# RWKV-7 recurrence: output products split in two places and accumulated in PSUM banks opened by products of zeros

## The chip, the cores and the metric

The kernel runs on one core of a Trainium2 chip. The metric is the device time of one execution in microseconds (us), a median over runs. TensorE (PE) does matrix products in the order of its program; VectorE (DVE), ScalarE (ACT) and GpSimd (POOL) do element-wise work; SyncE (SP) and ACT issue the DMA transfers. SBUF is the on-chip memory, PSUM the memory, in banks, into which PE writes its products.

## The reference

One hybrid decoder layer on 512 tokens of width 1024: a normalisation, one combined input projection, two mixers side by side (RWKV-7 with 16 heads of 64, and a sparse attention whose queries, keys and values come from the same projection), gates, an output projection and a gated MLP. The change is in the recurrence of the first mixer:

```python
def step(state, inp):
    r_t, w_t, k_t, v_t, a_t, b_t = inp
    sa = jnp.einsum('bhvk,bhk->bhv', state, a_t)
    state = (state * w_t[:, :, None, :] + sa[..., None] * b_t[:, :, None, :]
             + v_t[..., None] * k_t[:, :, None, :])
    return state, jnp.einsum('bhvk,bhk->bhv', state, r_t)
```

## The kernel before

All of it is one program; a scheduler decides in which order each engine's instructions stand.

**The recurrence.** It isn't stepped token by token. The 16 heads are two groups of eight (`g` = 0, 1), a group is four pairs (`GP` = 4, index `i`) of two halves (`h`), and the 512 tokens are eight chunks of 64 (`c`). For each group `recur` (L618) first finishes the inverse of each chunk's 64x64 triangular matrix from 32x32 blocks: `x` and `TT` are loaded from DRAM (L623 to L626), `mt` products (L635) are copied into `x` (ACT L639 for h = 0, DVE L641 for h = 1), and `mm` products (L649) are copied into `TT` (L654, L656). Then the chunks follow, each a chain:

- W: eight products of the state S (L687) into `xw`; DVE adds LV (L690). Chunk 0 has no state, its W is LV.
- TT: eight products of W (L701) into `xw` and `xs`; DVE (L703) and ACT (L704) copy the two halves into UV.
- BKT: eight products of UV (L710) into `xs`; DVE adds the decayed state SD (L715) and has the next state.

The outputs of a chunk are eight products of the state that it started from (L671, not for chunk 0) and eight of the chunk's own UV with GS (L674), both into `y`; each region of 128x64 is opened by its first product (`start=True`). `outputs` (L663) does them for chunk c-1, behind the W products of chunk c. Two `y` banks hold four chunks; behind every odd chunk ACT copies two half banks into YT (L678). The `y` banks take turns with `mt`'s and `mm`'s second halves in the PSUM tag `py`; `xw` and `xs` are in `px`.

**What runs beside it.** `drive` (L412) steps a list of other work (`fill`) and the spawned generators in turn. While group 1's recurrence runs, the fill is projections for the attention: `v`, then `khl` for the keys `ksp0` and `kwp0` (L823), then `qproj` q0 to q3 (L852); q4 and later follow in another list. Each is 24 products of 128x512 (L269, L270, L271: high times high, low times high, high times low) into one PSUM bank of the tag `pj`, which has two. `khl` empties its bank with two copies on ACT (L830, into `k0h` and `k1h`) and two subtractions on DVE (L831, into `k0l` and `k1l`). The weights come through three buffers each (`WB` = 3): raw, high part (ACT L109) and low part (POOL).

**Where the tiles lie.** Pool `rl` holds constants of the first mixer (`mask`, `rmask`, `sel`, `onesr`, `ltw`, `lta` and paddings). It is closed (`rtx.close()`, L813) right behind `rt1 = core(1)`, which only spawns group 1's recurrence. Pool `nk` (L814), with `k0h`, `k0l` and so on, is opened in its place. The framework orders an instruction that writes a reused place behind the last reader of the tile that lay there before.

Of the kernel before, what the change touches and what calls it, by code (L numbers as in the profile page):

```python
# [10 lines left out]
F32 = mybir.dt.float32  # L11
F32R = mybir.dt.float32r
AF = mybir.ActivationFunctionType
# [19 lines left out]
GP = 4  # L33
# [4 lines left out]
PADH, PADL, PADU, PADR = 96, 112, 80, 64  # L38
# [3 lines left out]
def hybrid_layer(ctx: ExitStack, tc: tile.TileContext, a, out, dbg=None, stop=None):  # L42
    nc = tc.nc
    te, ve, sc, po, sy = nc.tensor, nc.vector, nc.scalar, nc.gpsimd, nc.sync

    def pool(name, side="left", c=None):
        p = tc.tile_pool(name=name, bufs=1, side=side, reuse_waits="tile")
        if c is None:
            return p
        return c.enter_context(p)  # L50
# [6 lines left out]
    def pj(name):  # L57
        return ps.tile([128, 512], F32, tag="pj", name=name, bufs=2)

    def px(name):  # L60
        return ps.tile([128, 512], F32, tag="px", name=name, bufs=2)

    def py(name):
        return ps.tile([128, 512], F32, tag="py", name=name, bufs=2)
# [9 lines left out]
    def dump(name, ap):  # L74
        if dbg is not None and name in dbg:
            sy.dma_start(dbg[name], ap)

    rcx, rtx, rax, rhx, nctx, ncx = (ExitStack() for _ in range(6))
    rl = pool("rl", c=rtx)
# [218 lines left out]
    onesr = rl.tile([128, 128], F32R, name="onesr")  # L298
    ltw = rl.tile([128, S], F32R, name="ltw")
    lta = rl.tile([128, S], F32R, name="lta")  # L300
    rl.tile([128, PADR], F32, name="rpad1")
    lg1h = rc.tile([128, S], F32R, name="lg1h")
    lg1l = rc.tile([128, S], F32R, name="lg1l")
    lg2 = rc.tile([96, S], F32R, name="lg2")
# [29 lines left out]
    onesb = wp.tile([128, 128], F32, tag="raw", name="onesb", bufs=WB)  # L334
    sy.dma_start(onesb, a["onesb"])
    sc.activation(onesr, onesb, AF.Copy)
    dump("gates", gates)
    cp = pool("cp", "right", ncx)
    kcs = con.tile([128, 4, 2, 32], F32R, name="kcs")
# [278 lines left out]
    def recur(gr, g):  # L618
# [24 lines left out]
        for q in range(GP // 2):  # L643
            pm = [p_(f"mm{g}{q}{h}").rearrange(gi, i=2, j=32) for h, p_ in enumerate((px, py))]
            for i in range(2):
                for c in range(8):
                    for h in range(2):
                        lo, up = slice(64 * h, 64 * h + 32), slice(64 * h + 32, 64 * h + 64)
                        te.matmul(pm[h][lo, i, c], x1[up, 0, 2 * q + i, c], TT[up, 2 * q + i, c, 32:64], start=True,  # L649
                                  stop=True)  # L650
# [6 lines left out]
        YT = gr.YT = rh_.tile([128, 4, GP, 2, 64], F32, tag="XB", name=f"YT{g}", bufs=2)  # L657
        yield
        hs = [slice(0, 64), slice(64, 128)]
        iv = "p (i v) -> p i v"  # L660
        yps = [None]

        def outputs(c, Sc):  # L663
            if c % 4 == 0:
                yps[0] = [py(f"y{g}{c}{h}").rearrange("p (a i v) -> p a i v", i=GP, v=64) for h in range(2)]
            y = [b[:, c // 2 % 2] for b in yps[0]]
            for q in range(GP // 2):
                four = [(0, 2 * q), (1, 2 * q + 1), (0, 2 * q + 1), (1, 2 * q)]
                if c:
                    for h, i in four:  # L670
                        te.matmul(y[h][hs[(c + i) % 2], i], gr.AR[i][hs[h], 1, c * 64:(c + 1) * 64], Sc[hs[h], i],  # L671
                                  start=True, stop=False)
                for h, i in sorted(four):
                    te.matmul(y[h][hs[(c + i) % 2], i], gr.GS[:, 1 + i, c, h, :], gr.UV[:, c, i, h, :],  # L674
                              start=c == 0, stop=True)
            if c % 2:
                for h in range(2):
                    sc.activation(YT[:, c // 2, :, h], y[h], AF.Copy)  # L678

        St = None  # L680
        prev = None
        for c in range(8):
            xw, xs = px(f"xw{g}{c}"), px(f"xs{g}{c}")
            if c:
                for i in range(GP):
                    for h in range(2):
                        te.matmul(xw[hs[h], i * 64:i * 64 + 64], gr.AR[i][hs[h], 0, c * 64:(c + 1) * 64],  # L687
                                  St[hs[h], i], start=True, stop=True)
                W = rh_.tile([128, GP, 64], F32, tag="W", name=f"W{g}{c}", bufs=1)
                ve.tensor_tensor(W, xw[:, 0:64 * GP].rearrange(iv, v=64), gr.LV[:, :, c, :], op=OP.add)  # L690
                if c < 7:
                    SD = rh_.tile([128, GP, 64], F32, tag="SD", name=f"SD{g}{c}", bufs=1)
                    po.tensor_tensor(SD, St, gr.Dc[:, :, c, None].to_broadcast([128, GP, 64]), op=OP.mult)
            else:
                W = gr.LV[:, :, 0, :]
            if prev:
                outputs(*prev)
            yield
            for i in range(GP):
                for h in range(2):  # L700
                    te.matmul((xw, xs)[h][0:64, 256 + i * 64:320 + i * 64], TT[hs[h], i, c, :], W[hs[h], i], start=True,  # L701
                              stop=True)
            ve.tensor_copy(gr.UV[0:64, c, :, 0, :], xw[0:64, 256:512].rearrange(iv, v=64))  # L703
            sc.activation(gr.UV[0:64, c, :, 1, :], xs[0:64, 256:512].rearrange(iv, v=64), AF.Copy)  # L704
            yield
            prev = c, St
            if c < 7:
                for i in range(GP):
                    for h in range(2):
                        te.matmul(xs[hs[h], i * 64:i * 64 + 64], gr.BKT[i][:, c, hs[h]], gr.UV[:, c, i, h, :],  # L710
                                  start=True, stop=True)
                SN = rh_.tile([128, GP, 64], F32, tag="S", name=f"S{g}{c + 1}", bufs=2)
                xsv = xs[:, 0:64 * GP].rearrange(iv, v=64)
                if c:
                    ve.tensor_tensor(SN, xsv, SD, op=OP.add)  # L715
                else:
                    ve.tensor_copy(SN, xsv)
                St = SN
                yield
        outputs(*prev)  # L720

    def finish(gr, g):
        st = rh_.tile([128, 2, GP, 8], F32, tag="gst", name=f"gst{g}", bufs=1)
# [62 lines left out]
    def core(g):  # L786
        return spawn(invert(G[g], g), 0, 1.0), spawn(recur(G[g], g), RD, RR)
# [9 lines left out]
    for g in range(2):  # L797
        group_tiles(g)
        for i in range(GP):
            p = GP * g + i  # L800
# [276 lines left out]
    for p8 in range(8):  # L1077
        v = values(p8, os_[p8])
# [201 lines left out]
    with pool("ff") as ff:  # L1280
        ah = ff.tile([128, 22, S], F32R, name="ah")
        al = ff.tile([128, 22, S], F32R, name="al")
        for j in range(22):
            us = []
            for x in range(2):
                blk = 2 * j + x
                if blk < NU:
                    p = pu4[blk]
                    half_up(blk, 1)
                else:  # L1290
                    wh, wl = split_w(a["up"][blk], f"up{blk}")
                    p = pj(f"pu{blk}")
# [131 lines left out]
```

## Time and profile before

| | |
|---|---|
| median of three runs | 1249.28 us (1246.48 to 1250.75) |
| the profiled execution | 1244.42 us |
| its span, first to last instruction | 1242.4 us |
| mean granted TensorE clock | 0.977 of full |
| PE busy | 1191.7 us, 96% of the span |
| DVE, ACT, POOL busy | 48%, 46%, 45% |

The profile is one execution, and its times count from the start of its span. A row of the timeline gives start, length, engine, source line, operation, result <- operands, the shape, how many records, and in brackets the idle time ahead with what ended it. PE's records overlap, since products are pipelined: the distance from one start to the next is what a product costs. A float product is recorded twice, so eight products are 16 records. The granted clock is given as a share of full speed in stretches of time.

### The profile page before, as it was taken

How to read it: one execution, taken by the hardware profiler on the slowest of the kernel's cores; microseconds unless marked ns; L12 is line 12 of the kernel's file. 1: busy time of each engine (PE TensorE's matmuls, PEld its weight loads, DVE VectorE, ACT ScalarE, POOL GpSimd, SP SyncE). 2: the span in 40 equal slices, each digit the busy share in tenths (PEclk: the TensorE clock that was granted, in tenths of full speed). 3: DMA queues.
4: the chain of work that ended last, by engine and by line, in shares of the span. 5: the costliest groups of instructions: out<-in, count | busy, mean ns of one | idle time of the engine just before them, and what ended most of it. 6: DMA issues, size and time to landing. Idle time of an engine off the chain costs nothing.

```text
span 1242.4 us, 19852 instructions
## 1 busy us (share of the span) xinstructions
PE 1191.7 (96%) x7414; PEld 947.1 (76%) x7414; DVE 595.8 (48%) x1195; ACT 571.4 (46%) x1141; POOL 555.9 (45%) x519
## 2 busy tenths in 40 slices
PE   8999989999899999988999999999999999999997
PEld 6887778877677787766666766788888888888886
DVE  4225554623445393147788886745433333331103
ACT  5445553332545533246666664534444444443321
POOL 4357654433765551346323221441256565554440
PEclk8999999988989999889999999999999999999999
DMA  6522234630233347244542212761133333334421
GB/s 221 134 62 84 87 91 143 166 91 15 71 112 96 113 147 180 90 111 145 170 123 82 77 43 81 232 215 53 52 96 100 94 96 98 100 96 127 136 68 68
DMA packets 108610, 135.61 MB, mean 109 GB/s; under 512 B 46625, under 2 KB 49505, under 8 KB 108258
## 3 DMA queue, kind: packets, MB, share of 16 engines
q1 hardware_dynamic: 92306, 118.88, 32.3%
q10 hardware_dynamic: 16208, 15.47, 4.0%
q8 instruction: 58, 0.95, 0.3%
q14 instruction: 38, 0.31, 0.1%
HBM read 109.87 MB, written 21.23 MB: 106 GB/s over the span
## 4 chain that ended last, share of the span: by engine, by line
PE 53%; DVE 7%; issue 2%; POOL 2%; ACT 1%; DMA 1%; DVEq 0%; ACTq 0%; SPq 0%; POOLq 0%
PE pu L187 6%; PE pu L185 6%; PE pu L186 6%; PE dn L1156 3%; PE dn L1157 3%; PE dn L1155 3%; PE o L1021 3%; PE pt L113 3%; PE ub L1051 2%; DVE XL L608 2%; PE ub L1050 2%; PE ub L1049 2%; PE q L269 1%; PE wo L1227 1%; PE wo L1228 1%
## 5 line engine op out<-in xcount | busy, mean ns | idle before, releaser
L1297 DVE SCALAR_TENSOR_TENSOR u<-pu,cvec,u 128x511 f32<-128x511 f32 x44 | 33.0, 750 | 101.8 <-ACT u L1296 101.8
L1303 DVE TENSOR_TENSOR al<-u,ah 128x512 fp32r<-128x512 f32 x22 | 23.8, 1081 | 45.3 <-ACT ah L1302 45.3
L1301 POOL TENSOR_TENSOR u<-u,u 128x512 f32<-128x512 f32 x22 | 28.3, 1288 | 38.4 <-DVE u L1298 37.5
L1021 PE MATMUL o<-PT,vt 128*64 128x384 f32 (+3 forms) x256 | 42.8, 447 | 1.0 <-DVE PT L1009 1.0
L608 DVE TENSOR_TENSOR XL<-XL,TM 128x30 f32<-128x30 f32 (+14 forms) x60 | 42.1, 701 | 2.2
L606 DVE TENSOR_TENSOR TM<-XL 128x30 f32<-128x30 f32 (+14 forms) x60 | 23.9, 399 | 29.2 <-ACT XL L601 27.2
L1009 DVE COPY PT<-pt 128x384 f32<-128x384 f32 (+1 forms) x48 | 28.7, 598 | 15.3 <-PE pt L113 10.3
L1296 ACT ACTIVATE u<-pu,cvec 128x512 f32<-128x512 f32 x44 | 33.6, 763 | 5.2 <-PE pu L1261 5.2
L1007 ACT ACTIVATE PT<-pt 128x384 f32<-128x384 f32 (+1 forms) x48 | 25.0, 521 | 23.1 <-PE pt L113 16.1
L1298 DVE SCALAR_TENSOR_TENSOR u<-pu,cvec,u 128x510 f32<-128x510 f32 x44 | 33.0, 749 | 1.6
L567 PEld LDWEIGHTS g<-AR,KB 64*128 64x128 f32 x256 | 20.6, 187 | 14.1 <-issue 9.4
L567 PE MATMUL g<-AR,KB 64*128 64x128 f32 x256 | 23.9, 288 | 7.7 <-DVE KB L535 6.5
L1021 PEld LDWEIGHTS o<-PT,vt 128*64 128x64 f32 x256 | 15.4, 136 | 20.5 <-issue 10.4
L1203 DVE TENSOR_TENSOR p2tm<-dn,gb 128x512 f32<-128x512 f32 x4 | 2.8, 692 | 51.2 <-ACT p2jl L1201 51.2
L570 DVE TENSOR_TENSOR GS<-g,mask 128x512 f32<-128x512 f32 x32 | 20.7, 684 | 11.1 <-PE g L567 11.1
L704 ACT ACTIVATE UV<-xs 64x256 f32<-64x256 f32 x16 | 6.0, 377 | 41.3 <-PE xs L701 40.0
L294 DVE SCALAR_TENSOR_TENSOR V<-v,vec,V 128x511 f32<-128x511 f32 x8 | 6.0, 749 | 38.8 <-ACT V L293 38.8
L911 POOL TENSOR_SCALAR rh<-dist 128x512 f32<-128x512 f32 x16 | 10.1, 628 | 31.7 <-DVE stt L946 23.0
L1302 ACT ACTIVATE ah<-u 128x512 fp32r<-128x512 f32 x22 | 13.9, 633 | 21.6 <-POOL u L1301 21.6
L703 DVE COPY UV<-xw 64x256 f32<-64x256 f32 x16 | 6.6, 415 | 32.7 <-PE xw L701 18.3
L1227 PE MATMUL wo<-woh,mh 128*128 128x512 f32 x52 | 20.4, 393 | 0.0
L1228 PE MATMUL wo<-wol,mh 128*128 128x512 f32 x52 | 20.3, 390 | 0.0
(2787 smaller groups left out, 4305.4 us busy)
## 6 DMA issues: line engine op xcount, KB each, us to landing
gtd<-gt ACTq DMA_DIRECT2D x16, 256.0 KB, 2.1
qs<-qd SPq DMA_DIRECT2D x32, 128.0 KB, 3.2
g<-gtd SPq DMA_DIRECT2D x16, 256.0 KB, 3.6
xt<-in_x_dram SPq DMA_DIRECT2D x4, 512.0 KB, 5.4
bvd<-bv SPq DMA_DIRECT2D x8, 256.0 KB, 3.3
bvl<-bvd SPq DMA_DIRECT2D x8, 256.0 KB, 2.8
oad<-y SPq DMA_DIRECT2D x8, 256.0 KB, 3.4
t<-oad SPq DMA_DIRECT2D x8, 256.0 KB, 3.3
```

The costliest lines, as they stand in the source:

```text
L113: return te.transpose(o, i, ident)
L185: te.matmul(p, wh(k), mh(k), start=first and k == 0, stop=False)
L186: te.matmul(p, wh(k), ml(k), start=False, stop=False)
L187: te.matmul(p, wl(k), mh(k), start=False, stop=last and k == n - 1)
L567: te.matmul(gh[h][:, j * 128:(j + 1) * 128], KB[hs, c].rearrange("p s t -> p (s t)"), AR[hs, :, c * 64:(c + 1) * 64], start=True, stop=True)
L608: ve.tensor_tensor(XU[:, j + 1:32, 0:j], XU[:, j + 1:32, 0:j], tm, op=OP.add)
L1021: te.matmul(po8[e * 64:e * 64 + 64, j * 128:], vt[:, j, b * 256 + g * 64:b * 256 + g * 64 + 64], PT[j, e], start=False, stop=b == 1 and j ...
L1155: te.matmul(acc[half, t], sh[:, k, tsl], wh[kk], start=k == 0, stop=False)
L1156: te.matmul(acc[half, t], sh[:, k, tsl], wl[kk], start=False, stop=False)
L1157: te.matmul(acc[half, t], sl[:, k, tsl], wh[kk], start=False, stop=k == n - 1)
L1296: sc.activation(u, p, AF.Identity, scale=cvec[:, cv + 2:cv + 3], bias=cvec[:, cv + 3:cv + 4])
L1297: ve.scalar_tensor_tensor(u[:, 1:], p[:, :S - 1], cvec[:, cv + 1:cv + 2], u[:, 1:], op0=OP.mult, op1=OP.add)
```

## The change

`outputs` is replaced by two functions. `from_state(c)` does the eight state products of chunk c itself (L677), behind the W products of the same chunk (L695). `from_chunk(c)` does the eight products with GS (L683), behind the BKT products of the same chunk (L717). No region is opened by its own first product any more: `ybank` opens each of the two banks of four chunks with one product of zeros, 128x512 (L670), and all others accumulate. ACT copies whole banks (L687, 128x512) once per four chunks instead of half banks per two. The zeros are a new tile `zr` of 128x32 in pool `rl`, cut out of a padding there and filled by one ACT instruction (L338). `recur` yields once more at its end.

```diff
@@ -298,7 +298,8 @@
-    rl.tile([128, PADR], F32, name="rpad1")
+    zr = rl.tile([128, 32], F32R, name="zr")
+    rl.tile([128, PADR - 32], F32, name="rpad1")
@@ -334,6 +335,7 @@
     sc.activation(onesr, onesb, AF.Copy)
+    sc.activation(zr, onesb[:, 0:32], AF.Copy, scale=0.0)
@@ -658,27 +660,33 @@
-        yps = [None]
-
-        def outputs(c, Sc):
-            if c % 4 == 0:
-                yps[0] = [py(f"y{g}{c}{h}").rearrange("p (a i v) -> p a i v", i=GP, v=64) for h in range(2)]
-            y = [b[:, c // 2 % 2] for b in yps[0]]
-            for q in range(GP // 2):
-                four = [(0, 2 * q), (1, 2 * q + 1), (0, 2 * q + 1), (1, 2 * q)]
-                if c:
-                    for h, i in four:
-                        te.matmul(y[h][hs[(c + i) % 2], i], gr.AR[i][hs[h], 1, c * 64:(c + 1) * 64], Sc[hs[h], i],
-                                  start=True, stop=False)
-                for h, i in sorted(four):
-                    te.matmul(y[h][hs[(c + i) % 2], i], gr.GS[:, 1 + i, c, h, :], gr.UV[:, c, i, h, :],
-                              start=c == 0, stop=True)
-            if c % 2:
+        ys = {}
+
+        def ybank(c):
+            if c // 4 not in ys:
+                ys[c // 4] = []
                 for h in range(2):
-                    sc.activation(YT[:, c // 2, :, h], y[h], AF.Copy)
+                    b = py(f"y{g}{c}{h}")
+                    te.matmul(b, zr[:, 0:1].to_broadcast([128, 128]), zr[:, None, :].to_broadcast([128, 16, 32]), start=True, stop=False)
+                    ys[c // 4].append(b.rearrange("p (a i v) -> p a i v", i=GP, v=64))
+            return [b[:, c // 2 % 2] for b in ys[c // 4]]
+
+        def from_state(c, Sc):
+            y = ybank(c)
+            for h, i in [(0, 0), (1, 1), (0, 1), (1, 0), (0, 2), (1, 3), (0, 3), (1, 2)]:
+                te.matmul(y[h][hs[(c + i) % 2], i], gr.AR[i][hs[h], 1, c * 64:(c + 1) * 64], Sc[hs[h], i],
+                          start=False, stop=False)
+
+        def from_chunk(c):
+            y = ybank(c)
+            for h, i in itertools.product(range(2), range(GP)):
+                te.matmul(y[h][hs[(c + i) % 2], i], gr.GS[:, 1 + i, c, h, :], gr.UV[:, c, i, h, :],
+                          start=False, stop=c % 4 == 3 and i >= GP - 2)
+            if c % 4 == 3:
+                for h in range(2):
+                    sc.activation(YT[:, c // 4 * 2:c // 4 * 2 + 2, :, h], ys[c // 4][h], AF.Copy)
@@ -693,8 +701,8 @@
-            if prev:
-                outputs(*prev)
+            if c:
+                from_state(c, St)
@@ -703,7 +711,6 @@
-            prev = c, St
@@ -716,8 +723,8 @@
                 St = SN
-                yield
-        outputs(*prev)
+            from_chunk(c)
+            yield
```

The scheduler's order changes beyond these lines. The numbers in a name are those of the group and the chunk: `y140` is group 1, the bank opened at chunk 4, half 0; `xs14` is group 1, chunk 4.

On PE, in group 1, this stands behind the last product of `kwp0` before: q0's 24 products, of which the last three are shown, then thirteen of the 32x32 `mt` products, then q1.

```order
L269 MATMUL q0_4509<-hh_109,q0h1_4516 128x512
L270 MATMUL q0_4509<-hl_110,q0h1_4516 128x512
L271 MATMUL q0_4509<-hh_109,q0l1_4517 128x512
L635 MATMUL mt100_4589<-x11_4574 32x32 x13
L269 MATMUL q1_4555<-hh_109,q1h0_4556 128x512
L270 MATMUL q1_4555<-hl_110,q1h0_4556 128x512
L271 MATMUL q1_4555<-hh_109,q1l0_4557 128x512
```

The same place in the changed program, from the last product of `kwp0` on:

```order
L271 MATMUL kwp0_4466<-hh_109,kwp0l1_4474 128x512
L637 MATMUL mt100_4591<-x11_4576 32x32 x16
L637 MATMUL mt110_4627<-x11_4576 32x32 x16
L651 MATMUL mm100_4669<-TT1_3010,x11_4576 32x32 x16
L651 MATMUL mm110_4705<-TT1_3010,x11_4576 32x32 x16
L709 MATMUL xw10_4748<-LV1_3009,TT1_3010 64x64 x4
L637 MATMUL mt101_4592<-x11_4576 32x32 x16
L637 MATMUL mt111_4628<-x11_4576 32x32 x16
L651 MATMUL mm101_4670<-TT1_3010,x11_4576 32x32 x16
L651 MATMUL mm111_4706<-TT1_3010,x11_4576 32x32 x16
L670 MATMUL y100_4804<-zr_400 128x512
L683 MATMUL y100_4804<-UV1_3008,GS1_3003 64x64 x4
```

No product of q stands among them now, nor among those of chunks 0 to 3 that follow. The first comes in the middle of chunk 4, behind that chunk's TT products and half of its output products:

```order
L709 MATMUL xw14_5026<-W14_5036,TT1_3010 64x64
L709 MATMUL xs14_5027<-W14_5036,TT1_3010 64x64
L683 MATMUL y140_5040<-UV1_3008,GS1_3003 64x64 x4
L269 MATMUL q0_4511<-hh_109,q0h0_4512 128x512
L270 MATMUL q0_4511<-hl_110,q0h0_4512 128x512
L271 MATMUL q0_4511<-hh_109,q0l0_4513 128x512
```

All 96 products of q0 to q3 then stand in one run ahead of chunk 4's BKT products; 16 of q4 are interleaved with the rest of the recurrence (before, from chunk 4's BKT products to the end: 12 products of q).

On DVE the low parts of the keys stood ahead of the recurrence's copies (`x11<-mt101` follows two rows behind these):

```order
L831 TENSOR_TENSOR k0l_4028<-ksp0_4419,k0h_4027 64x512
L831 TENSOR_TENSOR k1l_4030<-ksp0_4419,k1h_4029 64x512
L831 TENSOR_TENSOR k0l_4028<-kwp0_4464,k0h_4027 64x512
L831 TENSOR_TENSOR k1l_4030<-kwp0_4464,k1h_4029 64x512
L841 SCALAR_TENSOR_TENSOR q0zl_4550<-q0_4509,q0zh_4549 128x512
L703 COPY UV1_3006<-xw10_4746 64x4x64
```

They now stand in chunk 4, behind its W; in brackets are the engines that a row waits for:

```order
L722 TENSOR_TENSOR S14_5014<-xs13_4975,SD13_4986 128x256 [waits PE_49,Activation_49,Pool_49]
L698 TENSOR_TENSOR W14_5036<-xw14_5026,LV1_3009 128x256 [waits DVE_49,PE_49]
L838 TENSOR_TENSOR k0l_4030<-ksp0_4421,k0h_4029 64x512 [waits PE_49,Activation_49]
L838 TENSOR_TENSOR k0l_4030<-kwp0_4466,k0h_4029 64x512 [waits Activation_49]
L711 COPY UV1_3008<-xw14_5026 64x4x64 [waits PE_49]
L838 TENSOR_TENSOR k1l_4032<-ksp0_4421,k1h_4031 64x512 [waits Activation_49]
L838 TENSOR_TENSOR k1l_4032<-kwp0_4466,k1h_4031 64x512 [waits Activation_49]
```

The first of them waits for PE besides ACT. `zr` begins 7432 bytes into pool `rl` (512 + 2048 + 8 + 256 + 512 + 2048 + 2048, the tiles ahead of it); in pool `nk` that place belongs to `k0l` (4096 to 8192), and the last reader of `zr` is the product `y141<-zr` at group 1's chunk 4. On ACT the copies into `k0h` and `k1h` (L837) stand behind the two bank copies of chunk 3 (L687), right behind `UV<-xs13`.

More of the change, by code (lines that the diff above doesn't have):

```diff
@@ L660, in recur @@
         iv = "p (i v) -> p i v"
-        yps = [None]
-        def outputs(c, Sc):
-            if c % 4 == 0:
-                yps[0] = [py(f"y{g}{c}{h}").rearrange("p (a i v) -> p a i v", i=GP, v=64) for h in range(2)]
-            y = [b[:, c // 2 % 2] for b in yps[0]]
-            for q in range(GP // 2):
-                four = [(0, 2 * q), (1, 2 * q + 1), (0, 2 * q + 1), (1, 2 * q)]
-                if c:
-                    for h, i in four:
-                        te.matmul(y[h][hs[(c + i) % 2], i], gr.AR[i][hs[h], 1, c * 64:(c + 1) * 64], Sc[hs[h], i],
-                                  start=True, stop=False)
-                for h, i in sorted(four):
-                    te.matmul(y[h][hs[(c + i) % 2], i], gr.GS[:, 1 + i, c, h, :], gr.UV[:, c, i, h, :],
-                              start=c == 0, stop=True)
-            if c % 2:
-                for h in range(2):
-                    sc.activation(YT[:, c // 2, :, h], y[h], AF.Copy)
+        ys = {}
+        def ybank(c):
+            if c // 4 not in ys:
+                ys[c // 4] = []
+                for h in range(2):
+                    b = py(f"y{g}{c}{h}")
[15 more added lines that the diff above has]
+                    sc.activation(YT[:, c // 4 * 2:c // 4 * 2 + 2, :, h], ys[c // 4][h], AF.Copy)
         St = None
-        prev = None
         for c in range(8):
```

## The prediction

> **What bounds the kernel now.** First the page: PE is busy nearly all of the span, and the chain that ended last runs over PE.
>
> ```profile
> span 1242.4 us, 19852 instructions
> PE 1191.7 (96%) x7414; PEld 947.1 (76%) x7414; DVE 595.8 (48%) x1195; ACT 571.4 (46%) x1141; POOL 555.9 (45%) x519
> PE 53%; DVE 7%; issue 2%; POOL 2%; ACT 1%; DMA 1%; DVEq 0%; ACTq 0%; SPq 0%; POOLq 0%
> ```
>
> So what the change does to waits of DVE or ACT counts only where PE runs out of other work. Then PE's timeline over group 1's recurrence:
>
> ```profile
> 471.74 0.39 PE L271 MATMUL kwp<-hh,kwp0l 128*128 128x512 f32 x1
> 472.24 0.47 PE L269 MATMUL q<-hh,q0h 128*128 128x512 f32 x1
> ...
> 477.57 0.39 PE L271 MATMUL q<-hh,q0l 128*128 128x512 f32 x1
> 478.92 1.00 PE L635 MATMUL mt<-x 32*32 32x32 f32 x26 [0.96 <-DMA x<-l]
> ...
> 485.70 2.21 PE L649 MATMUL mm<-TT,x 32*32 32x32 f32 x64
> ...
> 489.42 0.67 PE L701 MATMUL xw<-LV,TT 64*64 64x64 f32 x8
> 490.03 2.15 PE L635 MATMUL mt<-x 32*32 32x32 f32 x62
> ...
> 492.06 2.63 PE L649 MATMUL mm<-TT,x 32*32 32x32 f32 x63
> ...
> 496.83 1.12 PE L710 MATMUL xs<-UV,BKT 128*64 128x64 f32 x14 [0.47 <-ACT UV L704]
> ...
> 500.46 0.63 PE L270 MATMUL q<-hl,q2h 128*128 128x512 f32 x1
> 500.89 0.63 PE L271 MATMUL q<-hh,q2l 128*128 128x512 f32 x1
> ...
> 528.75 0.69 PE L710 MATMUL xs<-UV,BKT 128*64 128x64 f32 x16
> ...
> 543.13 0.45 PE L674 MATMUL y<-UV,GS 128*64 128x64 f32 x8
> ```
>
> The products of q fill every wait of the recurrence. They cost 0.23 us each (0.228 from start to start: q0's 24 from 472.24 to 477.57) and 0.43 us near 500 (from 500.46 to 500.89). There the granted clock was half; the columns behind the start:end are length, PE, PEld, DVE, ACT, POOL busy, then the clock:
>
> ```profile
> 490.00:492.00 2.00, 2.00 (x64) 1.98 (x63) 1.71 (x3) 0.13 (x1) 0.00 (x0) 1.00 0.39 149
> 492.00:494.00 2.00, 2.00 (x63) 2.00 (x60) 1.39 (x2) 0.00 (x0) 0.00 (x0) 0.85 0.39 139
> 494.00:496.00 2.00, 2.00 (x29) 1.82 (x27) 0.69 (x1) 0.00 (x0) 0.00 (x0) 0.50 0.00 0
> ...
> 502.00:504.00 2.00, 2.00 (x6) 1.54 (x6) 0.00 (x0) 0.26 (x1) 0.00 (x0) 0.59 0.45 122
> ```
>
> ```profile
> 282.00:285.00 3.00, 3.00 (x36) 2.21 (x38) 1.64 (x4) 0.58 (x1) 1.64 (x2) 0.50 0.02 5
> 285.00:289.00 4.00, 4.00 (x43) 3.19 (x40) 1.97 (x4) 0.20 (x2) 0.73 (x1) 0.55 0.00 0
> ```
>
> From 490 to 494 PE was busy throughout, with 32x32 products, and the clock fell to half (0.85 over a stretch that began full: at 493.4). It came back in 502 to 504 (0.59: at 503.6), over 3 us into a run of wide products. Small 64x64 products at 282 to 285, without a gap, kept it at half. So a row of small products loses the clock, and the wide ones bring it back.
>
> **The change, part by part.** What decides is a side effect. `zr` lies where `k0l` will lie, so DVE's first write into `k0l` waits for the last zero product, in chunk 4 of group 1. Until then `ksp0` and `kwp0` hold both `pj` banks and no product of q can begin. The order shows it: PE has no wide product from `kwp0`'s last to the middle of chunk 4, but the two zero products of the first `y` banks. The 96 products of q0 to q3 cost the same, but behind the chain instead of in its gaps. So the sum follows the chain alone. Its prices:
>
> ```profile
> 473.79 1.56 SPq L623 DMA_DIRECT2D x<-l  x1
> ...
> 480.05 0.30 SPq L625 DMA_DIRECT2D TT<-xd  x1
> ```
>
> ```profile
> DMA to landing us min/median/max: 3.9/4.7/5.3
> ```
>
> ```profile
> L639 ACT ACTIVATE x<-mt x4: 587/587/588, 249.6 to 484.2; 32x512 f32<-32x512 f32 x4
> L641 DVE COPY x<-mt x4: 696/697/698, 257.6 to 492.3; 32x512 f32<-32x512 f32 x4
> ```
>
> ```profile
> 284.43 0.80 PE L687 MATMUL xw<-S,AR 64*64 64x64 f32 x10
> ...
> 287.69 0.37 PE L701 MATMUL xw<-W,TT 64*64 64x64 f32 x1
> ...
> 288.50 0.27 PE L701 MATMUL xs<-W,TT 64*64 64x64 f32 x1
> ...
> 292.93 0.27 PE L701 MATMUL xw<-W,TT 64*64 64x64 f32 x1
> ...
> 294.43 0.69 PE L710 MATMUL xs<-UV,BKT 128*64 128x64 f32 x16
> ...
> 295.81 0.68 PE L687 MATMUL xw<-S,AR 64*64 64x64 f32 x16
> ```
>
> ```profile
> 292.26 0.42 DVE L690 TENSOR_TENSOR W<-xw,LV 128x256 f32<-128x256 f32 x1 [0.21 <-PE xw L687]
> 293.64 0.42 DVE L703 COPY UV<-xw 64x256 f32<-64x256 f32 x1 [0.95 <-PE xs L701]
> 295.26 0.42 DVE L715 TENSOR_TENSOR S<-xs,SD 128x256 f32<-128x256 f32 x1 [1.21 <-PE xs L710]
> ```
>
> 1. *The start.* `kwp0` ends at 472.1. `mt` can't begin before 478.92: there it waited for `x<-l` (issued 473.79), and that load doesn't move. With q0 gone PE idles 6.8 us, twice the 3.4 us of small products (490.03 to 493.4) that cost it the clock above, so I take half clock from here. The second group of `mm` (492.06) took 2.63 us, the first 2.21 for about as many at full clock. The 0.45 us more fell on what lay behind 493.4, 1.3 us: a factor of about 1.6, so a group of 64 takes 3.5 us at half. `mt` of the first half: 478.9 to 482.4. `mm` needs TT (issued 480.05, 4.7 to land: 484.8) and ends at 488.3; ACT's copy with its hand-over 0.8, 489.1; chunk 0's first products 1.1, 490.2; `mt` and `mm` of the other half, 497.2; DVE's copy 0.9, hidden by two zero products and chunk products between them, 1.4 in all, 498.6; 1.1 for `xs`, 0.6 for UV, 1.2 for BKT, 0.7 for S. W of chunk 1 can begin at 502.2.
>
> 2. *A chunk at half clock.* W: ten records took 0.80, with 0.05 for each of six more 1.1. TT: 287.69 to 288.77, 1.08. BKT: fourteen took 1.12, so 1.2. Between them 0.05 to DVE's W, 0.42, 0.25 until the products start (292.68 to 292.93); 0.04, 0.42 and 0.25 for UV; 0.14 (295.12 to 295.26), 0.42 and 0.13 for S. Sum 5.5 us. The output products lie inside these waits. Three chunks: 502.2 + 16.5 = 518.7.
>
> 3. *Chunk 4.* q0 stands behind a part of its output products. W 1.1, then two zero products and eight state products, about 1.3 (these cover W's 0.7), TT 1.1, UV 0.7, the chunk products 0.4: 523.3. DVE's UV copy now stands behind two `k0l` rows, which wait for ACT's two bank copies of chunk 3 and for `k0h`:
>
> ```profile
> L830 ACT ACTIVATE k0h<-ksp 64x512 fp32r<-64x512 f32 x1 | 0.6, 576 | 0.0
> ```
>
> ```profile
> L831 DVE TENSOR_TENSOR k0l<-ksp,k0h 64x512 fp32r<-64x512 f32 x1 | 0.7, 675 | 0.0
> ```
>
> A bank copy taken at this 0.6, that chain is 0.2 + 1.2 + 0.6 + 0.7 + 0.7, so 3.4 us from 518.7; with 0.7 for UV and 0.3 for products it ends at 523.1. Either way q0 begins near 523.3.
>
> 4. *The run.* 96 x 0.228 = 21.9 us, and the first 4 us at half clock (an estimate from the over 3 us above) lose 2. BKT of chunk 4 starts at 523.3 + 23.9 = 547.2, against 528.75: 18.45 late.
>
> 5. *The rest of the recurrence.* It took 14.8 us (528.75 to 543.58). There are 16 products of q in place of 12 (+0.9) and fewer changes between 64-row and 128-row products (-0.4): +0.5. Behind it PE waits for a load that hangs on the recurrence's end:
>
> ```profile
> 550.30 0.60 PE L898 MATMUL pc<-kcs,qs 128*128 128x64 f32 x4 [1.28 <-DMA qs<-qd]
> ```
>
> So the lateness passes through. The ten products of q fewer by then stand partly in that gap and in the score's gaps behind it: 0, at most 10 x 0.23 = 2.3.
>
> 6. *Group 0.* Here the fill (projections of the first mixer) stays between the products. Four zero products at 0.23, +0.9. The trace has none with a broadcast operand; I take the nearest 128x512 row, half-clock 0.43 as the upper end. The regrouping: chunk products behind BKT and state products behind W save some four changes of row count per chunk, at most 0.1 us each (eight records behind such a change, 543.13, took 0.45; eight of the sixteen at 295.81 half of 0.68), in seven chunks 0 to -2.8, halved because the fill already separates many: -1.4. Together -0.5 (from -1.9 to +1.7). The added fill of `zr`, the fewer copies on ACT and the extra yield lie beside PE: 0; without that cover under 1 us.
>
> Sum: +18.45 + 0.5 - 0.5 = +18.45 us, rounded 18.5. The profiled execution of 1244.42 would become 1262.9; it lies 4.86 under the median, and 1249.28 + 18.5 = **1267.8**. Uncertain are the factor 1.6 (at 2 the three groups behind 484.8 take 2.7 more), a chunk's 5.5 (0.5 either way, 2 in all), the tail's 2.3 and group 0: 1263 to 1274 for this case alone.
>
> **Rivals.** *The clock holds or returns during the small products.* Steps 1 to 3 at full speed: groups of 2.2, chunk 0 of 0.67 + 0.6 + 0.7 + 0.7, BKT at 495.8, W1 at 496.5, chunks of 4.1 (0.68 + 0.62 + 0.69 and the same 2.1 of hand-overs), chunk 4 at 508.8. Here DVE's chain of 4.3 decides: q0 at 513.1, BKT 4 at 535.0, 6.2 late. The sum is +6.2, 1255.5. Against it are the rows of 490 to 494 and of 282 to 285. The Trainium skill ("TensorE: Matmul & The Clock Gate", Part 1) says that the clock halves after an idle window of about 3.4 us and returns after about 3.4 us of sustained work, which speaks for a return inside the chunks if these count as work. The trace agrees on the length (over 3 us of wide products) but not for small ones, which kept half clock with PE busy 3.00 of 3.00. I give it 0.17.
>
> *Not slower: the regrouping pays everywhere.* It needs that full clock, plus all bounds on the good side: 0.4 us off each of fourteen chunks (-5.6), and group 0 no longer falling to half at 282 to 289 (7 us at half, -3.3). 6.2 - 5.6 - 3.3 = -2.7, or 1246.6. The point from which it decides: chunks 1 to 3 shorter than 4.1 us without any fill. Only 0.05.
>
> *Longer still.* The clock stays half into the run for 10 us instead of 4 (+3 on 1267.8), or the weights' conversions for q1 to q3, which now queue behind ACT's copies, starve the run (each half needs ACT 0.6 and POOL's low part within 12 x 0.23 = 2.7 us, so little; 5 us if it does for two of the halves): 1271 to 1279 with the upper bounds above. Chance 0.06.
>
> **How the numbers follow.** Forecast 0.72, full clock 0.17, other side 0.05, longer 0.06. The range goes from just under the full-clock case, 1254, to 1277. About 0.3% (3.7 us) can be told from no change: faster 0.02, within 0.04, slower 0.94.
>
> **What would show it.** Between `kwp0`'s last product and chunk 4 no product of q; PE idle some 7 us ahead of `mt`, the clock 0.5 from there to the run of q0, chunks of 5.5 us, BKT of chunk 4 near 547 and the recurrence ending near 562. Wrong it would be if q0 stood among the first chunks, if `mt` came earlier than 478.9, or if the clock column read 1.00 in chunks 1 to 3; and if the rest (up to 470 and behind 570) moved by more than 2 us.

## The result, and the profile after

The changed kernel takes 1252.19 us (median, 1249.1 to 1260.37) against 1246.64 before (1241.11 to 1255.38), the two run side by side. The ratio is 1.0056, with a 95% interval from 1.0041 to 1.0070: 7.0 us slower (5.1 to 8.7; the medians alone differ by 5.6, and all costs below go by the ratio). The forecast was 18.5 us slower, so the direction was right and the size was not.

The page of the changed kernel: PE still fills the span, which is 9.5 us longer (1251.9 against 1242.4).

```profile
span 1251.9 us, 19863 instructions
PE 1192.9 (95%) x7422; PEld 950.1 (76%) x7422; DVE 598.2 (48%) x1195; ACT 571.8 (46%) x1134; POOL 555.8 (44%) x519
PE 44%; DVE 2%; issue 1%; ACT 1%; POOL 1%; DMA 0%; DVEq 0%; POOLq 0%; ACTq 0%
```

PE's timeline over group 1's recurrence, changed kernel: the last product of `kwp0`, `mt`, `mm`, BKT of chunk 0, W of chunks 1 to 4, the first product of q0, BKT of chunk 4, the last outputs.

```profile
466.28 0.39 PE L271 MATMUL kwp<-hh,kwp0l 128*128 128x512 f32 x1
474.89 3.43 PE L637 MATMUL mt<-x 32*32 32x32 f32 x61 [8.22 <-DMA x<-l]
...
478.27 3.44 PE L651 MATMUL mm<-TT,x 32*32 32x32 f32 x61
...
493.43 1.12 PE L717 MATMUL xs<-UV,BKT 128*64 128x64 f32 x16 [0.47 <-ACT UV L712]
...
495.15 0.80 PE L695 MATMUL xw<-S,AR 64*64 64x64 f32 x10 [0.17 <-DVE S L724]
...
500.37 1.01 PE L695 MATMUL xw<-S,AR 64*64 64x64 f32 x14
...
504.63 0.51 PE L695 MATMUL xw<-S,AR 64*64 64x64 f32 x10 [0.23 <-DVE S L722]
...
508.44 0.68 PE L695 MATMUL xw<-S,AR 64*64 64x64 f32 x16 [0.21 <-DVE S L722]
...
512.97 0.50 PE L269 MATMUL q<-hh,q0h 128*128 128x512 f32 x1 [0.51 <-DVE k1l L838]
...
534.95 0.69 PE L717 MATMUL xs<-UV,BKT 128*64 128x64 f32 x16
...
547.82 0.69 PE L683 MATMUL y<-UV,GS 128*64 128x64 f32 x16
```

What the order showed happens on the chip: no product of q from 466 to 513, 8.2 us of idle PE ahead of `mt`, and q0 waits for DVE's `k1l`, the last of the keys' rows. The clock (seventh figure behind the start:end) over the same place:

```profile
466.00:475.00 9.00, 0.78 (x6) 0.35 (x6) 0.00 (x0) 2.52 (x2) 1.26 (x1) 0.79 0.99 232
475.00:490.00 15.00, 14.94 (x265) 14.51 (x264) 2.62 (x5) 2.35 (x4) 0.00 (x0) 0.50 0.49 74
...
494.00:502.00 8.00, 7.15 (x132) 6.28 (x128) 2.11 (x5) 0.38 (x1) 1.24 (x2) 0.51 0.01 2
502.00:512.00 10.00, 7.33 (x178) 5.88 (x178) 4.14 (x9) 3.20 (x7) 1.24 (x2) 1.00 0.07 16
```

It is half from about 471 on (0.79 over the first row), inside the idle stretch as forecast, but full again from 502, eleven us before the first product of q. Step 1 of the prediction also has two loads in it, which stand as follows on SP's queue:

```profile
470.22 0.52 SPq L625 DMA_DIRECT2D x<-l  x1
...
471.68 1.59 SPq L627 DMA_DIRECT2D TT<-xd  x1
```

Both moved ahead: before, `x<-l` was issued at 473.79 and `TT<-xd` 6.3 us behind it, at 480.05; now the second follows the first by 1.5 us, since `x<-xd`, which stands between them on the queue, comes 0.6 us behind `x<-l` and not 3.9.

To compare many kernels, the span is cut at four events: the start of group 0's first `mt` product, the end of the last product of `kwp0`, the end of the last output product of group 1, and the start of the last closing `dn` product. For the changed kernel the first stands in the rows of tile `mt`, the fourth in those of tile `dn`:

```profile
L637 PE MATMUL mt<-x x256: 191/220/255, 250.1 to 486.4; 32*32 32x32 f32 x128
```

```profile
L1162 PE MATMUL dn<-h2h,ah x32: 389/389/389, 1223.3 to 1244.3; 128*128 128x512 f32 x32
```

"Up" is from `mt` of group 0 to the end of `kwp0`, "recurrence" from there to the last outputs (466.67 to 548.51 here), "tail" from there to that `dn` product. All kernels, with the experiments that follow:

| kernel | ratio to before (95%) | up | recurrence | tail |
|---|---|---|---|---|
| before | 1 | 223.7 | 71.5 | 691.2 |
| changed | 1.0056 (1.0041 to 1.0070) | 216.6 | 81.8 | 695.8 |
| late reader, chunk 4 | 1.0100 (1.0068 to 1.0131) | 220.2 | 84.4 | 694.0 |
| late reader, chunk 0 | 1.0021 (0.9998 to 1.0045) | 223.6 | 77.6 | 689.9 |
| zeros, old places, zr in rl | 1.0104 (1.0071 to 1.0137) | 220.8 | 84.7 | 694.4 |
| zeros, old places, zr in hp | 1.0022 (0.9997 to 1.0047) | 220.8 | 72.5 | 694.1 |
| changed, zr among the constants | 1.0070 (1.0045 to 1.0095) | 222.2 | 70.0 | 701.4 |
| zeros, old places, zr among the constants | 1.0096 (1.0063 to 1.0128) | 221.3 | 72.3 | 703.2 |
| changed, zr in hp | 0.9981 (0.9951 to 1.0010) | 216.7 | 70.3 | 697.1 |
| the same again | 1.0012 (0.9992 to 1.0033) | 219.6 | 70.2 | 695.5 |
| the same, four zero products a bank | 1.0009 (0.9987 to 1.0031) | 222.9 | 70.6 | 697.5 |
| copies only | 0.9972 (0.9941 to 1.0003) | 221.1 | 73.3 | 693.6 |
| changed, warm products | 1.0044 (1.0024 to 1.0063) | 219.2 | 78.9 | 696.1 |
| changed, wide products in gaps | 1.0085 (1.0059 to 1.0112) | 216.4 | 82.6 | 695.8 |
| changed, both | 1.0071 (1.0043 to 1.0099) | 217.1 | 81.8 | 696.1 |
| before, 128 bytes of shift | 1.0055 (1.0033 to 1.0077) | 222.6 | 69.1 | 698.3 |

One profiled execution stands behind each stretch, and the kernel that was run twice ("changed, zr in hp" and "the same again") differs by 2.9 us in "up"; what counts is where kernels of one kind stand together. The recurrence doesn't hold the same work in all of them: kernels with q beside the chain have 120 to 126 recorded products of q in it (122 before), those without 110 to 113 (113 changed); the others follow in the tail. One of the twelve executions of the kernel with copies only took 1646.63 us at a granted clock of 0.65 and is not in its ratio.

### The profile page after: what moved, and what is told of

It is laid out like the page before. It is cut to its first block, busy times and chain, and to the rows that moved or that the text cites. A ratio compares the mean times of both kernels' runs of the same rounds, so it can differ in the third digit from the quotient of the medians.

```text
span 1251.9 us, 19863 instructions
## 1 busy us (share of the span) xinstructions
PE 1192.9 (95%) x7422; PEld 950.1 (76%) x7422; DVE 598.2 (48%) x1195; ACT 571.8 (46%) x1134; POOL 555.8 (44%) x519
## 5 line engine op out<-in xcount | busy, mean ns | idle before, releaser
L608 DVE TENSOR_TENSOR TM<-XL 128x30 f32<-128x30 f32 (+14 forms) x60 | 23.9, 398 | 29.8 <-ACT XL L603 27.8
L1016 DVE COPY PT<-pt 128x384 f32<-128x384 f32 (+1 forms) x48 | 28.7, 598 | 15.3 <-PE pt L113 11.8
L1028 PEld LDWEIGHTS o<-PT,vt 128*64 128x64 f32 x256 | 15.3, 136 | 20.7 <-issue 10.1
L701 POOL TENSOR_TENSOR SD<-S,Dc 128x256 f32<-128x256 f32 x12 | 7.5, 622 | 49.2 <-DVE S L724 23.8
L1210 DVE TENSOR_TENSOR p2tm<-dn,gb 128x512 f32<-128x512 f32 x4 | 2.8, 692 | 51.2 <-ACT p2jl L1208 51.2
```

Of the source, the lines that this page charges most:

```text
L1028: te.matmul(po8[e * 64:e * 64 + 64, j * 128:], vt[:, j, b * 256 + g * 64:b * 256 + g * 64 + 64], PT[j, e], start=False, stop=b == 1 and j ...
```

## The experiments

### Where zr lies

The first run moves `zr` into the pool of constants.

```diff
-    zr = rl.tile([128, 32], F32R, name="zr")
-    rl.tile([128, PADR - 32], F32, name="rpad1")
+    zr = con.tile([128, 32], F32R, name="zr")
+    rl.tile([128, PADR], F32, name="rpad1")
```

> The changed kernel with zr in the pool of constants that stays open to the end, and nothing else. The order puts q0 back ahead of mt. Place theory (the whole loss comes from zr's place): group 1's recurrence takes 71.5 us from the end of kwp0 to its end as before, not 81.9, and if the 7 us that the changed kernel had gained ahead of kwp0 belong to the regrouping, they stay: 1238 to 1243 against 1246.6 before. Rival (those 7 us are chance and the regrouping is worth nothing): 1245 to 1248. Rival (the place isn't the cause): about 1252.

It took 1254.75 us, ratio 1.0070 (1.0045 to 1.0095), above all three forecasts. The order had q0 ahead of `mt` again and the recurrence took 70.0 us, yet the kernel was no faster than the changed one: what was won there came back elsewhere, in part in the last stage, far from the recurrence. Two runs put the zeros into the kernel before, with the output products left in their places and banks copied whole, `zr` once in `rl` and once among the constants.

```diff
-                yps[0] = [py(f"y{g}{c}{h}").rearrange("p (a i v) -> p a i v", i=GP, v=64) for h in range(2)]
+                yb = [py(f"y{g}{c}{h}") for h in range(2)]
+                for b in yb:
+                    te.matmul(b, zr[:, 0:1].to_broadcast([128, 128]), zr[:, None, :].to_broadcast([128, 16, 32]), start=True, stop=False)
+                yps[0] = [b.rearrange("p (a i v) -> p a i v", i=GP, v=64) for b in yb]
...
-            if c % 2:
+            if c % 4 == 3:
                 for h in range(2):
-                    sc.activation(YT[:, c // 2, :, h], y[h], AF.Copy)
+                    sc.activation(YT[:, c // 4 * 2:c // 4 * 2 + 2, :, h], yps[0][h], AF.Copy)
```

> The kernel before with its output products where they were, but banks opened by zero products, all else accumulating, banks copied once per four chunks, and zr in the pool that is closed, as in the change: so the place of zr without the regrouping. Place theory with a gain of the regrouping: the loss of the recurrence and its tail (10 + 5) without the gain ahead of it, 1257 to 1263. Rival (the regrouping is worth nothing): 1250 to 1255, like the changed kernel.

> As the run before, but with zr in the pool that stays open: only the zero products, the accumulation and the copies of whole banks are left of the change. Every theory: within 2 us of 1246.6, since eight products of 0.23 us are all that is added on PE; the slower end if the two zero products delay W's chain.

They took 1258.73 (1.0104) and 1257.25 us (1.0096, 1.0063 to 1.0128). The second missed every expectation. Its milestones show where the time went: the last stage was as long as in the first run, 5.6 us longer than in every kernel here without a shift. There the tile shifts all that lies behind it by 128 bytes. So `zr` was put where nothing moves, into the padding behind `hh` and `hl`, which stay open past the last product of q:

```diff
-    hp.tile([128, PADH], F32, name="hpad")
+    zr = hp.tile([128, 32], F32R, name="zr")
+    hp.tile([128, PADH - 32], F32, name="hpad")
```

> The changed kernel with zr in place of a part of another padding, that of the pool which holds the normalised stream (hh, hl) and stays open past the last product of q. Unlike the run with zr in the pool of constants this moves no other tile, and q0 stands ahead of mt again. In the two runs with zr among the constants the last stage, from the first 128x256 product of pu to the first dn product that closes it, took 346.2 us against 340.6, so 5.6 us of their loss were laid on the shifted places. Theory of places: the last stage is back at 340.6, and the time is the 1254.75 of that run less 5.6, 1249 (1247 to 1251). Rival (the shift is not the cause): 1253 to 1256. Then against the changed kernel (1252.2) zr's place in the closed pool is worth 3 us, not 18.

> The kernel before with its output products in their old places, banks opened by zero products and copied whole, and zr in that other padding, so without a shift and without a wait of the keys. By the run with zr among the constants less 5.6: 1251.6 (1249 to 1254), so the zeros and whole copies cost 3 to 8 us by themselves. Rival (the shift cost more than the last stage shows): 1246 to 1248. Against the run with zr in the closed pool and the old places (1258.7) the difference is what the place of zr costs there: 7 by the first, 12 by the second.

With the change 1243.97 us (0.9981), below both forecasts; with the old places 1247.0 (1.0022), as the rival had it, by which the shift cost more than the last stage shows. Timeline of PE, changed kernel with `zr` in `hp`: the end of `kwp0`, `mt` behind q0 with 2.3 us of idle time, the end at full cover.

```profile
464.88 0.39 PE L272 MATMUL kwp<-hh,kwp0l 128*128 128x512 f32 x1
...
473.41 1.00 PE L637 MATMUL mt<-x 32*32 32x32 f32 x26 [2.31 <-DMA x<-l]
...
534.85 0.69 PE L683 MATMUL y<-UV,GS 128*64 128x64 f32 x16
```

The recurrence takes 70.3 us against 81.8. Compared with the changed kernel, the place of `zr` is worth 0.0059 (1.0056 less 0.9997, the mean of both runs of this kernel), 7 us; with the old places 0.0082 (1.0104 less 1.0022), 10 us. Between the two profiled executions (1253.92 and 1242.29 us) the difference is larger, 11.6, nearly all of it the 11.5 of the recurrence; the ratio goes by all executions.

The smallest test of the cause adds one product to the kernel before, which reads another tile of the closed pool late:

```diff
+            if (g, c) == (1, 4):
+                te.matmul(xw[64:128, 256:320], onesr[:, 0:64].bitcast(F32), onesr[:, 0:64].bitcast(F32), start=True, stop=True)
             if prev:
                 outputs(*prev)
```

> The kernel before with one 64x64 product added: in group 1 at chunk 4 it reads onesr, another tile of the pool that is closed, and writes into a part of the xw bank that nothing reads. No zeros, no regrouping, no other copies. Place theory: the order loses q ahead of chunk 4 as in the change, and the time rises by what zr's place cost in both pairs (1252.2 against 1244.0, 1258.7 against 1247.0): 8 to 12 us, 1254 to 1258; the recurrence from the end of kwp0 takes 82 to 85 us. By the sum on record it would be +18.5, 1264. Rival (the cost in the pairs comes from something that goes with the zeros): 1245 to 1248.

1258.32 us, ratio 1.0100, at the upper end of what the theory of the place gave: one product of 64x64 costs 12.5 us (8.5 to 16.3). Its timeline has the pattern of the changed kernel, without zeros or regrouping:

```profile
469.31 0.39 PE L271 MATMUL kwp<-hh,kwp0l 128*128 128x512 f32 x1
475.78 3.43 PE L635 MATMUL mt<-x 32*32 32x32 f32 x61 [6.09 <-DMA x<-l]
...
500.22 1.12 PE L687 MATMUL xw<-S,AR 64*64 64x64 f32 x16
...
506.08 1.12 PE L687 MATMUL xw<-S,AR 64*64 64x64 f32 x16
...
515.64 0.80 PE L269 MATMUL q<-hh,q0h 128*128 128x512 f32 x1
...
553.60 0.45 PE L674 MATMUL y<-UV,GS 128*64 128x64 f32 x8
```

With the reader at chunk 0 (`(1, 0)` in the same line):

> As the run before, but with the reader at chunk 0, so that q0 may begin behind the first mm products. Place theory: the idle stretch ahead of mt and the half clock in mt stay (7 us idle, 1.2 us more for each of one or two groups), chunks 0 to 4 have their cover again: 4 to 7 us slower, 1250 to 1253. If chunks 1 to 4 without cover were what costs: under 3 us.

1249.88 us, 1.0021 (0.9998 to 1.0045), 2.6 us and not clearly slower: not the 4 to 7 us of the first case, but the second, by which chunks 1 to 4 without cover are what costs. The recurrence takes 77.6 us, 6.1 more than before. The idle stretch ahead of `mt` (6.54 us) and half clock in both first groups stand there as with the reader at chunk 4:

```profile
479.33 3.43 PE L635 MATMUL mt<-x 32*32 32x32 f32 x61 [6.54 <-DMA x<-l]
482.71 3.44 PE L649 MATMUL mm<-TT,x 32*32 32x32 f32 x61
```

So a good part of the cost in the recurrence comes with the four chunks that have no cover: 77.6 against 84.4 us. Whether it is the missing cover or the half clock in them that costs, these two runs don't separate.

### Is it the clock?

Thirty-two products of zeros fill the idle stretch ahead of `mt`:

```diff
+        if g:
+            wb = py("warm1")
+            for j in range(WARM):
+                te.matmul(wb, zr[:, 0:1].to_broadcast([128, 128]), zr[:, None, :].to_broadcast([128, 16, 32]), start=j == 0, stop=j == WARM - 1)
```

> The changed kernel with 32 more zero products (7.3 us at full clock) put into the idle stretch between kwp0 and mt in group 1, into a bank that nothing reads. Clock theory (most of the 10 us lost in the recurrence is half clock after the idle stretch): mt and mm take 2.2 us a group, not 3.4, and chunks 0 and 1 run at full clock, 5 to 8 us back, 1244 to 1248. Rival (the missing cover of q is what costs): no change, 1251 to 1254. If products of zeros don't count for the clock, the same.

1251.43 us (1.0044), not separable from the changed kernel, as the rival had it. The recurrence is 2.9 us shorter. The first group (`mt`) ran at full clock, the third (`mt` of the other half) was at half again:

```profile
467.70 7.71 PE L635 MATMUL warm<-zr 128*128 128x512 f32 x32
476.31 2.18 PE L642 MATMUL mt<-x 32*32 32x32 f32 x64 [0.91 <-DMA x<-l]
...
482.68 3.46 PE L642 MATMUL mt<-x 32*32 32x32 f32 x61
```

Then up to six zero products a chunk were put into the chain's gaps in chunks 0 to 3 of group 1, accumulating nothing into an open bank, without and with the thirty-two:

```diff
+        def wide(c, n):
+            if g and c < 4:
+                ybank(c)
+                b = ys[c // 4][0].rearrange("p a i v -> p (a i v)")
+                for _ in range(n):
+                    te.matmul(b, zr[:, 0:1].to_broadcast([128, 128]), zr[:, None, :].to_broadcast([128, 16, 32]), start=False, stop=False)
...
                 from_state(c, St)
+                wide(c, 2)
...
             sc.activation(gr.UV[0:64, c, :, 1, :], xs[0:64, 256:512].rearrange(iv, v=64), AF.Copy)
+            wide(c, 3)
...
+            if c != 3:
+                wide(c, 1)
             from_chunk(c)
```

> The changed kernel with 23 more zero products in group 1's chunks 0 to 3, two behind W, three behind TT and one behind BKT, accumulating nothing into a y bank: they fill the gaps that q's products filled before, but do no work. If the missing cover costs by the clock (small products with gaps keep it at half), the clock comes back in chunk 0 or 1 and stays: chunk 1 takes 4.2 us, not 5.2, at most 2 us gained, 1250 to 1252. If the clock comes back by itself anyway: same or up to 2 us slower, 1252 to 1255. In neither case near the 1244 of zr's other place: the time of q behind the chain stays lost.

> The same wide products and the 32 ahead of mt together. By the clock theory of the sum on record (half clock from the idle stretch to the run of q, worth 18.45 less 6.2, so 12 us): 1243 to 1246. By the traces so far (half clock cost mt, mm and chunks 0 and 1, of which the 32 products alone gave back 3 us of the recurrence's time): 1248 to 1251, and of the loss most stays, since it is the chain without cover.

1255.37 (1.0085) and 1254.03 us (1.0071): both slower than the changed kernel if anything, the second above both of its forecasts, though the clock did come back. With both, the clock was full from about 491, and PE was busy throughout from 494 to 502:

```profile
490.00:494.00 4.00, 3.17 (x71) 2.68 (x72) 0.42 (x1) 0.38 (x1) 0.62 (x1) 0.86 0.00 0
494.00:502.00 8.00, 8.00 (x137) 5.54 (x128) 2.23 (x6) 0.76 (x2) 0.62 (x1) 1.00 0.01 2
```

The recurrence took 81.8 us, as in the changed kernel. Bringing the clock back with products that do no work pays for itself at best.

What half clock costs by itself stays open. The test isn't clean: with both, the last two of the four groups of `mt` and `mm` still ran at half (3.46 and 3.44 us), the one ahead of them in part (2.74), and the zero products made chunks 1 and 2 take 4.7 us, where chunk 1 took 4.2 at full clock with the thirty-two alone. By the rows, half clock cost the changed kernel some 6 us (an estimate: 3.4 less 2.2 in four groups, 5.2 less 4.2 in chunk 1; chunk 0 left out, and if no load ends later). The 12 us that the sum on record gives it were priced for half clock up to the run of q, and it ended at 502. That the clock has a share is seen between executions too: the changed kernel was granted 0.973 on average, the kernel before 0.979 to 0.982 in the five sets beside the experiments, and the slower executions of the changed kernel have the lower clock (1260.37 us at 0.964, 1250.18 at 0.979). That the rest is the work of q, which now stands behind the chain, is argued and not shown.

### The zeros, the copies, the regrouping

The kernel before with whole-bank copies alone (the second hunk of the diff of the zeros above):

> The kernel before with nothing changed but the copies into YT: whole banks once per four chunks, as in the change; no zero products, each region opened by its own first product. If the late whole-bank copies (they hold the y banks and delay the group norm) are what makes the stretch between the first score products and the first value products longer (37.6 us before, 41 to 45 in every run so far), they show it here: 1250 to 1253, and that stretch above 41. If the zero products are: 1245 to 1247 and 37 to 39.

1242.76 us (0.9972), the stretch from the first score product to the first value product 38.5 us (550.0 to 588.5) against 37.6 (550.3 to 587.9) before: the copies cost no time that shows. Four zero products to open each bank, with `zr` in `hp`:

```diff
-                    te.matmul(b, zr[:, 0:1].to_broadcast([128, 128]), zr[:, None, :].to_broadcast([128, 16, 32]), start=True, stop=False)
+                    for j in range(4):
+                        te.matmul(b, zr[:, 0:1].to_broadcast([128, 128]), zr[:, None, :].to_broadcast([128, 16, 32]), start=j == 0, stop=False)
```

> The changed kernel with zr in the other padding (1244.0), each y bank opened by four zero products in place of one: 24 more products of 128x512, 5.5 us of PE at full clock. If a zero product costs its own 0.23 us: 1249 to 1250. If it costs more (the zeros with the whole copies were 3 us slower than nothing, the copies alone 3 us faster, so up to 0.7 us a product): 1255 to 1260. If they lie in PE's gaps: 1244 to 1246.

1246.96 us (1.0009) against 0.9997 for one product a bank: 24 products cost 1.5 us, within the intervals nothing, and by no means more than their own 5.5 us. So the change's eight cost under 2 us, if each costs what these do. Last, whether the change with `zr` in `hp` beats the kernel before:

> The changed kernel with zr in the padding that stays, once more, to see whether it beats the kernel before: the first time 1243.97, ratio 0.9981 with an interval that holds 1. If the regrouping (5 us faster in two pairs) outweighs the zeros and copies (2.7 us slower in one run), the ratio lies again at 0.996 to 0.999; if the first time was chance, at 1.000 to 1.002.

1244.81 us (1.0012), so by its forecast the first result was chance. With 0.9981 the first time, it is the same as before within 0.2%, and clearly better than the change as it was made.

### The shift

> The kernel before with an unused tile of 128 bytes a partition among the constants, which moves all that lies behind it on that side; no instruction is added. By the runs with zr there (1254.75 against 1243.97 without the shift, 1257.25 against 1247.0) 10 to 11 us slower, 1256 to 1257, with the last stage at 346.2 us against 340.6. Rival (the shift alone does nothing): 1245 to 1247.

The edit is one unused tile, `con.tile([128, 32], F32, name="shift")`, ahead of `gates`. 1252.75 us (1.0055, 1.0033 to 1.0077): 6.9 us slower with no instruction added, less than the 10 to 11 forecast. Between the kernels with `zr` among the constants and those with it in `hp` lie 0.0073 (changed) and 0.0074 (old places), 9 us; the intervals allow that the shift is all of it, but don't show it. The stretch from the first 128x256 product of `pu` to the first closing `dn` product, before and then with the shift:

```profile
872.90:1213.50 340.60, 339.25 (x1571) 284.17 (x1570) 105.44 (x133) 140.67 (x231) 178.66 (x140) 1.00 0.33 97
```

```profile
873.40:1219.60 346.20, 344.82 (x1570) 284.53 (x1569) 106.18 (x133) 140.74 (x231) 179.17 (x140) 1.00 0.30 95
```

As many products (1571 and 1570 recorded), the same full clock, PE 5.6 us longer. The same stretch takes 346.4 us in both kernels with `zr` among the constants too, and 340.7 to 340.8 in all kernels without a shift (by starts of 0.1 us).

## Why the prediction was wrong, by its steps

- **The side effect** (`zr` under `k0l`, the keys' rows late, q behind the chain) is right and is the cause of the loss: q0 came behind `k1l` in chunk 4 as forecast, one late reader of that pool makes it in the kernel before, and another place for `zr` takes it away. What it costs in time is 7 us in the changed kernel and 10 to 12 us with the old grouping, not 18.
- **Step 1, the start, 23.3 us from `mt` to W of chunk 1:** 20.3 (474.89 to 495.15). The idle stretch and half clock came (groups took 3.4 us for the 3.5 estimated), but `mm` did not wait for TT: it follows `mt` at 478.27. The landing at 484.8 was carried over from the kernel before by its absolute time, 2.4 us behind `mt`'s end; but TT's load was issued 8.4 us earlier here (471.68), and `x<-l`, of which the text says that it doesn't move, 3.6 us earlier. 3.0 us too much; against it the idle stretch ahead of `mt` took 8.2 us, not 6.8.
- **Step 2, three chunks at half clock, 16.5 us:** 13.3 (495.15 to 508.44). The price of a chunk was right where the clock was half: 5.2 from 495.15 to 500.37, and 5.9 from 500.22 to 506.08 in the kernel with the late reader. But it came back at 502 in the changed kernel, among small products with gaps, and the next two chunks took 4.3 and 3.8 us. **This is the step that failed**, the largest part of the miss: that small products keep the clock at half up to the run of q. With step 4 it makes 3.2 + 1.9 = 5.1 of the 8.6 us by which the recurrence was priced too long; steps 1 and 5 make most of the rest. The two rows of 282 to 289 in the prediction don't show that. Those stretches hold 128x512 products among the small ones, and the second row, 0.55, has the clock coming back inside it, at about 288.6:

```profile
283.70 0.80 PE L271 MATMUL k<-hh,k5l 128*128 128x512 f32 x1
...
285.69 0.79 PE L269 MATMUL k<-hh,k5h 128*128 128x512 f32 x1
```

```profile
288.00:288.50 0.50, 0.50 (x15) 0.50 (x12) 0.50 (x2) 0.00 (x0) 0.23 (x1) 0.50 0.00 0
288.50:289.00 0.50, 0.50 (x7) 0.42 (x6) 0.42 (x2) 0.15 (x1) 0.50 (x1) 0.90 0.00 0
```

Where the clock did stay half, in the kernel with the zeros in old places and `zr` in `rl`, the three chunks took 17.2 us, close to the price:

```profile
497.15 0.80 PE L692 MATMUL xw<-S,AR 64*64 64x64 f32 x10 [0.17 <-DVE S L722]
...
514.32 1.12 PE L692 MATMUL xw<-S,AR 64*64 64x64 f32 x16
```

```profile
502.00:514.00 12.00, 11.00 (x171) 9.33 (x172) 2.84 (x7) 0.76 (x2) 1.33 (x3) 0.50 0.01 3
```

- **Step 3, chunk 4, 4.6 us:** 4.5 (508.44 to 512.97), DVE's keys deciding as in the full-clock rival.
- **Step 4, the run, 23.9 us:** 22.0 (512.97 to 534.95), since the clock was full already: the 2 us for half clock weren't lost.
- **Step 5, the rest, +0.5 on 14.8:** 13.6 (534.95 to 548.51). Regrouped chunks are shorter by more than the products of q added. Together the recurrence from `kwp0`'s end took 81.8 us where the steps make 90.4 (6.8 + 23.3 + 16.5 + 4.6 + 23.9 + 15.3).
- **Step 6, the regrouping, -0.5 in all:** perhaps too little, but the gain isn't shown. Six executions with the change's grouping have "up" from 216.4 to 219.6 us, the six others without a shift 220.2 to 223.7; but four zero products a bank make it 222.9 with that grouping, the shift 222.2, and one kernel alone spans 2.9 us. The recurrence with cover is 70.0 to 70.6 against 71.5 to 73.3, but 69.1 in the kernel before with the shift. The tail takes part back (695.5 to 697.1 against 689.9 to 694.4). As the last stage is the same in all of these, that lies ahead of it; in the changed kernel 9 products of q more (2 us) are a part of it. In time the gain shows where the chain is bare, 1.0056 (1.0041 to 1.0070) against 1.0104 (1.0071 to 1.0137), the intervals just apart; but there the clock came back at 502 in the one profile and at about 515 in the other, so it need not be the grouping. With cover, 0.9997 against 1.0022, it isn't clear. What makes "up" shorter and the tail longer was not tried; both lie mostly in stages that the change doesn't touch, in an order that the scheduler lays anew.
- **The rivals:** the time fell on the full-clock rival's +6.2 by luck, not by its mechanism: the clock was half for some 31 us (471 to 502). From the end of `kwp0` to q0 the steps make 51.2 us and the rival 41.0; it took 46.3, half way between. That q0 (512.97) and chunk 4's BKT (534.95) stand where the rival put them comes from "up", which was 7 us shorter. The two profiled executions differ by 9.5 (10.3 in the recurrence, less 7.1 in "up", plus 4.6 in the tail, and 1.7 of a later start); over all executions it is 7.0. The Trainium skill ("TensorE: Matmul & The Clock Gate", Part 1) has the clock return after about 3.4 us of sustained activity. The wide products of zeros fit that here: with both kinds the clock was back at about 491.1, 3.9 us behind the first of six at 487.24. Small products don't: PE was busy 14.94 of 15.00 us from 475 to 490 at half clock.
- **What would show it:** q0 was not among the first chunks, the clock read 0.5 up to chunk 1, but 1.00 in chunks 2 and 3, which the text had named as a sign of error; so had it a move of more than 2 us outside that stage, and "up" moved by 7. A third such sign came too: `mt` began at 474.89, earlier than 478.9. It would have been safer to price the clock's return as a range, full from any chunk on (each of steps 2 to 4 then has two values), than as two cases with 0.72 and 0.17.

What brings the clock back among small products is not settled: after the idle stretch it stayed half to 502 in the changed kernel, to about 509 with the late reader at chunk 4 (0.91 over 508 to 512), and to about 515 with the zeros in old places, always among small products.

## What to carry to other kernels

A tile's last reader sets when the place under it may be written, so a new reader late in the program belongs into a pool that closes later; one product cost 12 us here because its pool's successor held two PSUM banks' worth of other work. When cover moves away from a chain, price the chain bare and the cover behind it, and treat the clock in it as unknown rather than as the value that one stretch of the trace shows. Work out a load's landing from what stands ahead of it on its queue, not from its time in the old trace. Before a tile is added for any reason, see which tiles it shifts: put it into existing padding.

## What the hardware showed unexpectedly

Moving tiles by 128 bytes a partition made the kernel 6.9 us slower (1.0055) without an instruction more; the rows above show 5.6 us of it in a stage that is PE alone, at full clock. It sits in the 984 recorded 128x512 products of `pu` there, which read `h2h` and `h2l`: their groups have means of 394 to 396 ns with the shift and 389 to 391 before, 5 us in all. The `dn` products of that stage, which read `ah` and `al`, have 389 to 392 in both. One group of `pu`, with the shift and before:

```profile
L185 PE MATMUL pu<-h2h,up7h 128*128 128x512 f32 x8 | 3.2, 396 | 0.0
```

```profile
L185 PE MATMUL pu<-h2h,up7h 128*128 128x512 f32 x8 | 3.1, 389 | 0.0
```

Which operand's place matters was not tried. And products of zeros kept the clock up like others: with thirty-two of them ahead, the first `mt` group took 2.18 us, not 3.43.
